# Earlier accumulating transfers, a seven-product group in the first block, and a twelfth group with sums made ahead, in a one-core decoder layer

## The chip, the core and the metric

The kernel runs on one core of one Trainium2 chip. A core has a matrix engine (TensorE, PE in the profile), a vector engine (VectorE, DVE), a scalar engine (ScalarE, ACT), a general engine (GpSimd, POOL), a sequencer that here issues nearly all loads (SyncE, SP), and sixteen engines for transfers (DMA) which all queues share. Each engine works through its own list of instructions in the order in which the program was written down, and waits on semaphores for the others. The metric is device microseconds of one execution, lower is better.

## The reference

One decoder layer over 256 tokens of width 2048, all in float32: a half feed-forward with a residual and a norm, two token mixers side by side (retention in chunks, and attention over a window with sinks), their gated mix, a second half feed-forward, and a gated embedding. Cut to what matters here:

```python
D_MODEL, SEQ, D_FF = 2048, 256, 5632

def swiglu(x, w_gu, w_down):
    g, u = jnp.split(x @ w_gu, 2, axis=-1)
    return (jax.nn.silu(g) * u) @ w_down

def reference(x, p, positions, ...):
    h = x
    h = layer_norm(alpha * h + 0.5 * swiglu(h, w_ffn1_gu, w_ffn1_down), ...)
    rq, rk, rv, rg, aq, ak, av, gate_r, gate_a = jnp.split(h @ w_in, SPLIT_POINTS, axis=-1)
    ro = head_group_norm(retention_chunkwise(rotary(rq), rotary(rk) * DK ** -0.5, rv), ret_gn_g)
    ret_branch = (jax.nn.silu(rg) * ro) @ w_ret_out
    att_branch = sliding_window_attention_sinks(rotary(aq), rotary(ak), av, att_sinks) @ w_att_out
    mixed = (jax.nn.sigmoid(gate_r) * ret_branch + jax.nn.sigmoid(gate_a) * att_branch) @ w_mix_out
    h = layer_norm(alpha * h + mixed, ...)
    h = layer_norm(alpha * h + 0.5 * swiglu(h, w_ffn2_gu, w_ffn2_down), ...)
    ple = jax.nn.sigmoid(h @ w_ple_gate) * (p @ w_ple_proj)
    return layer_norm(alpha * h + ple, ...)
```

`w_gu` is 2048 by 11264 and `w_down` 5632 by 2048, once for each feed-forward. Every weight is read once, so the work is a stream of weights past 256 tokens.

## The kernel before

**Three matmuls for one product.** Float32 numbers are split in two parts, hi and lo, of a shorter type (`F32R`). One product of two tiles is then three matmuls: lo of the activations with hi of the weights (L431), hi with hi (L432), hi of the activations with lo of the weights (L433). A matmul has 128 rows of tokens on one side and 512 columns of weights on the other.

**Weights.** A weight chunk is 128 by 1024 numbers, 512 KB (tile `r...`, loaded by SP at L119). The split is a copy on ACT to `h...` (L105) and a subtraction on DVE to `l...` (L106). In the tile names `lf1_gu_2_1_6`, the letter is lo, `f1_gu` is the gate and up projection of feed-forward 1, block 2, half 1 (0 is gate, 1 is up), pair 6 of features.

**Blocks and units.** The gate and up projections are made in 11 blocks (0 to 10) of 512 gate and 512 up columns. A block is a sum over eight units, one for each pair of feature tiles. A unit has one of four kinds:

- P: two chunks, each split as above. 8 products, 24 matmuls.
- F: like P, but the second chunk is *folded*: its lo is not subtracted on DVE. ACT writes minus the raw chunk into it (L169, one multiplication), POOL issues a transfer that adds the raw chunk to it (L170, `lf_gu<-rf_gu`, 512 KB), and ACT copies hi (L171). The accumulating transfer takes the place of the rounding subtraction that DVE would have made.
- S: the *seven*: seven products in place of eight, in the manner of Strassen, 21 matmuls. DVE makes four sums of weight halves (L226 to L229, tiles `u` and `v`), and three splits follow on ACT and DVE (`h`, `b`, `hu`, `hv` and the same with `l`). A block with sevens needs four further banks of PSUM (`f1..s0` to `s3`) and, at its end, the *fold*: a copy on ACT (`eve`, L549) and four operations on DVE (`evw`, `eve`, L550 to L553), then the four sums that add in the block's own banks (L1056), the activation (L1057) and the product. A block without sevens ends with activation (L1062) and product (L1064) alone. The activations for sevens are sums too (`sums`, L504 to L507, split into `f1fh` and `f1fl`), made once.
- D: a seven whose sums of weights were made in an earlier stage, stored in DRAM (`sums_ahead`) and loaded again.

Feed-forward 1 is PPPPPPPP in block 0 and FFSSFSSP in the other ten. The units' pairs are fixed, sevens are pairs 0 to 3, and folded chunks are pairs 4, 5 and 6. Feed-forward 2 has five sevens in each of its blocks 1 to 7, one or two of them of kind D, and four sevens in blocks 8 to 10. The down projections are made in two parts with lists of their own, `FIRST_DOWN` and `SECOND_DOWN`, one letter for each of 22 units.

**What sets the order.** Units stand in one list, `plan`. `fill()` runs whenever a unit has been multiplied: it loads the next units and makes them (the split) as long as slots are free (`room["slots"]`, of a pool of 46) and the units waiting amount to less than 45 (made) or 90 (loaded) units of matmul time, 12 for a chunk and 21 for a seven. So the lists of SP, ACT, DVE and POOL follow the order of `plan`, some units ahead of the matmuls, and a folded chunk's multiplication, its accumulating transfer and its hi copy are written at one place (`Folded.make`), in turn with the units around it. In block 0 of feed-forward 1 the four chunks of `x` are loaded between the weights (`first_chunk`), and the number of slots is raised to 24 before its seventh unit. Work for other stages (`sums_ahead`) is put in small steps between the units (`lazy`).

Of the kernel before, what the change touches and what calls it, by code (L numbers as in the profile page):

```python
# [38 lines left out]
SLOTS = 46  # L39


SEVEN = (0, 1, 2, 3)

AHEAD = {1: (4, 5), 2: (4,), 3: (4, 5), 4: (4,), 5: (4, 5), 6: (4,), 7: (4, 5)}
AHEAD_SLOTS = 36

DELAY = 1

SEVEN_DOWN = (6, 7, 8, 9)

FIRST_DOWN = "PPPPPPFFSFSPSFSPSFSSPS"
SECOND_DOWN = "PPPSPSPSFSPSFSSPSPPPPP"
LEAD = 4

# [8 lines left out]
def layer(ctx: ExitStack, tc: tile.TileContext, io):  # L63
# [87 lines left out]
        def make(self):  # L151
            self.chunk.make()

    class Folded:

        loads, makes, keeps, time = 1, 2, 2, 12

        def __init__(self, key):  # L160
            self.key = key

        def load(self, **how):
            self.chunk = Chunk(self.key, **how)

        def make(self):
            c = self.chunk
            c.make_hi()
            act.mul(c.lo, c.raw, -1.0)  # L169
            pool.dma_start(c.lo, c.raw, accum_op=ALU.add)  # L170
            act.copy(c.hi, c.raw)  # L171

    class Turn:

# [141 lines left out]
    def fill(must=False):  # L316

        while True:
            queued = sum(u.time for u in ready)
            left = room["slots"] - room["used"]  # L320
            wanted = must and not ready or not room["quiet"] and queued < room["ahead"]
            if loaded and wanted and loaded[0].makes <= left:
                u = loaded.pop(0)
                u.make()
                room["used"] += u.keeps - u.loads
                ready.append(u)
                continue
            first = loaded[0] if loaded else plan[0] if plan else None
            queued += sum(u.time for u in loaded)
            if plan and queued < room["far"] and plan[0].loads + first.makes <= left:  # L330
                u = plan.pop(0)
                u.load()
                room["used"] += u.loads
                loaded.append(u)
                continue
            return

    def make_next():
# [4 lines left out]
        ready.append(u)  # L343

    def take(key):
        if not ready:
            fill(True)
        u = ready.pop(0)
        assert u.key == key, (u.key, key)
        return u  # L350
# [102 lines left out]
    def block_units(units, keys):  # L453

        for kind, p in units:
            if kind == "P":
                plan.extend(Single(keys(n, p)) for n in range(2))
            elif kind == "F":
                plan.extend(of(keys(n, p)) for n, of in enumerate((Single, Folded)))
            else:  # L460
                plan.append((Seven if kind == "S" else Prepared)(keys(0, p), keys(1, p)))

# [511 lines left out]
    def ffn(name, i, ht, norm, keep, residual, keepers, away):  # L974
# [33 lines left out]
        for j in range(KF // 4):  # L1008
# [22 lines left out]
            def before(u, j=j, offset=KD // 2 - len(units)):  # L1031
                u += offset
                if j == 0 and norm is None and u % 2 == 0:
                    first_chunk(u // 2)
                    if u == 6:
                        slots_for_weights(24)
                    if u == 2:
                        load_constants()
                if j == 0 and u == 7:
                    for g in sorted({p // 2 for p in SEVEN}):  # L1040
                        hi, lo = (slot([P, 8, P], F32R, f"{name}f{w}{g}") for w in "hl")
                        made[g] = seven_forms(keep[g], hi, lo)
                    if name == "f2":
                        g = AHEAD[1][0] // 2
# [169 lines left out]
    def mixers(ht, norm, residual, keepers, away):  # L1214
# [295 lines left out]

        made = {}
        forms = lambda p: made[p // 2](p % 2)
        lazy.append(sums_ahead(ahead[6:9], 2, 2))
        slots_for_weights(18)
        sig = []
        for j in range(4):
# [76 lines left out]

        lhs = lambda k: of_pairs(mix_t, k)
        slots_for_weights(16)
        lazy.append(sums_ahead(ahead[9:], 3, 2))

        def residual_added(blk, ps):
            for t in range(2):
# [344 lines left out]
```

## Time and profile before

| | |
|---|---|
| median of 3 runs | 2230.45 us (2227.97 to 2230.84) |
| profiled execution | 2230.62 us, of which the profile's span is 2228.6 us |
| PE, share of the span busy | 100% (2218.5 us) |
| DVE | 90% (2004.0 us) |
| ACT | 65% (1439.0 us) |
| POOL | 2% (50.9 us) |
| mean traffic to and from the memory | 233 GB/s |
| granted clock of the matrix engine | 0.999 |

A page of the profile gives busy times, the chain of work that ended last, and groups of instructions. The list of waits names, for each engine, what a waiting instruction was released by. A timeline row has the start, the duration, the engine, the line, the operation, its output and inputs, and in square brackets how long the engine sat idle before it and what ended that. A matmul row says 0.39 us, but matmuls overlap: what counts is the distance between the starts of two of them. Of the queues, q1 carries the loads that SP issues, and q0 the accumulating transfers that POOL issues.

### The profile page before, as it was taken

How to read it: one execution, taken by the hardware profiler on the slowest of the kernel's cores; microseconds unless marked ns; L12 is line 12 of the kernel's file. 1: busy time of each engine (PE TensorE's matmuls, PEld its weight loads, DVE VectorE, ACT ScalarE, POOL GpSimd, SP SyncE). 2: the span in 40 equal slices, each digit the busy share in tenths (PEclk: the TensorE clock that was granted, in tenths of full speed). 3: DMA queues.
4: the chain of work that ended last, by engine and by line, in shares of the span. 5: the costliest groups of instructions: out<-in, count | busy, mean ns of one | idle time of the engine just before them, and what ended most of it. 6: DMA issues, size and time to landing. Idle time of an engine off the chain costs nothing.

```text
span 2228.6 us, 29103 instructions
## 1 busy us (share of the span) xinstructions
PE 2218.5 (100%) x10140; PEld 1838.9 (83%) x10140; DVE 2004.0 (90%) x2624; ACT 1439.0 (65%) x1677; POOL 50.9 (2%) x65
## 2 busy tenths in 40 slices
PE   9999999999999999999999999999999999999998
PEld 8888888888888888888788888888888888888887
DVE  6999999989998789789999888779999999999977
ACT  6777777777565545557865567466766677765653
POOL 0000000000000000000000000000000000000000
PEclk9999999999999999999999999999999999999999
DMA  9988998976686889757976568888999999666871
GB/s 321 250 264 252 249 263 241 269 227 217 228 305 234 298 283 338 203 179 232 291 233 226 184 203 321 316 302 266 301 301 295 300 248 276 209 233 221 309 283 68
DMA packets 302075, 570.51 MB, mean 256 GB/s; under 512 B 98652, under 2 KB 103388, under 8 KB 301928
## 3 DMA queue, kind: packets, MB, share of 16 engines
q1 hardware_dynamic: 291880, 536.71, 72.3%
q0 software_dynamic: 8064, 29.36, 7.0%
q10 hardware_dynamic: 1984, 2.58, 0.4%
q8 instruction: 79, 1.29, 0.2%
q14 instruction: 68, 0.56, 0.1%
HBM read 487.32 MB, written 31.46 MB: 233 GB/s over the span
## 4 chain that ended last, share of the span: by engine, by line
PE 93%; DMA 3%; DVE 2%; issue 1%; ACT 0%; SPq 0%; ACTq 0%; POOL 0%; DVEq 0%; POOLq 0%
PE rqk L382 3%; PE f2g L431 3%; PE f2g L433 3%; PE f2g L432 3%; PE f1g L431 2%; PE f1g L433 2%; PE f1g L432 2%; PE f2u L431 2%; PE f2u L433 2%; PE f2u L432 2%; PE f1u L433 2%; PE f1u L431 2%; PE f1u L432 2%; PE aqk L382 2%; PE f2e L431 1%; PE f1e L431 1%
## 5 line engine op out<-in xcount | busy, mean ns | idle before, releaser
L106 DVE TENSOR_TENSOR lf_gu<-rf_gu,hf_gu 128x1024 fp32r<-128x1024 f32 (+1 forms) x225 | 267.7, 1210 | 22.1 <-ACT hf_gu L105 21.1
L105 ACT CAST hf_gu<-rf_gu 128x1024 fp32r<-128x1024 f32 (+1 forms) x225 | 228.7, 1039 | 22.1 <-DMA rf_gu<-in_f_gu 21.5
L106 DVE TENSOR_TENSOR lw_in_f<-rw_in_f,hw_in_f 128x1024 fp32r<-128x1024 f32 x140 | 167.8, 1219 | 15.0 <-ACT hw_in_f L105 15.0
L106 DVE TENSOR_TENSOR lf_down<-rf_down,hf_down 128x1024 fp32r<-128x1024 f32 x130 | 155.7, 1220 | 12.9 <-ACT hf_down L105 11.1
L105 ACT CAST huf_gu<-uf_gu 128x1024 fp32r<-128x1024 f32 x76 | 80.1, 1053 | 125.4 <-DVE uf_gu L227 109.4
L105 ACT CAST hf_down<-rf_down 128x1024 fp32r<-128x1024 f32 x130 | 132.7, 1049 | 30.5 <-DMA rf_down<-in_f_down 21.3
L105 ACT CAST hw_in_f<-rw_in_f 128x1024 fp32r<-128x1024 f32 x140 | 140.4, 1049 | 2.3 <-PE gt L433 1.6
L105 ACT CAST hvf_gu<-vf_gu 128x1024 fp32r<-128x1024 f32 x76 | 80.1, 1054 | 32.4 <-DVE vf_gu L229 30.5
L106 DVE TENSOR_TENSOR luf_gu<-uf_gu,huf_gu 128x1024 fp32r<-128x1024 f32 x76 | 92.6, 1218 | 0.0
L106 DVE TENSOR_TENSOR lvf_gu<-vf_gu,hvf_gu 128x1024 fp32r<-128x1024 f32 x76 | 92.6, 1218 | 0.0
L431 PE MATMUL f1g<-hf_gu,xt 128*128 128x512 f32 x232 | 90.8, 391 | 0.0
L433 PE MATMUL f1g<-lf_gu,xt 128*128 128x512 f32 x232 | 90.5, 390 | 0.0
L432 PE MATMUL f1g<-hf_gu,xt 128*128 128x512 f32 x232 | 90.5, 390 | 0.0
L431 PE MATMUL f2g<-hf_gu,ht 128*128 128x512 f32 x211 | 82.2, 390 | 0.0
L433 PE MATMUL f2g<-lf_gu,ht 128*128 128x512 f32 x211 | 82.1, 389 | 0.0
L432 PE MATMUL f2g<-hf_gu,ht 128*128 128x512 f32 x211 | 82.1, 389 | 0.0
L433 PE MATMUL f1u<-lf_gu,xt 128*128 128x512 f32 x192 | 75.0, 391 | 1.2 <-DMA lf_gu<-rf_gu 1.2
L431 PE MATMUL f1u<-hf_gu,xt 128*128 128x512 f32 x192 | 74.7, 389 | 0.0
L432 PE MATMUL f1u<-hf_gu,xt 128*128 128x512 f32 x192 | 74.7, 389 | 0.0
L170 POOL DMA_DIRECT2D lf_gu<-rf_gu x42 | 36.4, 867 | 1641.2 <-DMA rf_gu<-in_f_gu 1017.6
L105 ACT CAST huf_down<-uf_down 128x1024 fp32r<-128x1024 f32 x32 | 33.7, 1054 | 60.7 <-DVE uf_down L227 58.7
L1057 ACT ACTIVATE eve<-eve 128x1024 f32<-128x1024 f32 x20 | 21.2, 1061 | 67.3 <-DVE eve L1056 67.3
(1512 smaller groups left out, 6978.3 us busy)
## 6 DMA issues: line engine op xcount, KB each, us to landing
rf_gu<-in_f_gu SPq DMA_DIRECT2D x361, 512.0 KB
rf_down<-in_f_down SPq DMA_DIRECT2D x176, 512.0 KB
rw_in_f<-in_w_in_f SPq DMA_DIRECT2D x148, 512.0 KB
lf_gu<-rf_gu POOLq DMA_DIRECT2D x42, 512.0 KB, 8.2
rw_rv<-in_w_rv SPq DMA_DIRECT2D x32, 512.0 KB
rw_ret<-in_w_ret SPq DMA_DIRECT2D x32, 512.0 KB
rw_mix<-in_w_mix SPq DMA_DIRECT2D x32, 512.0 KB
rw_pg<-in_w_pg SPq DMA_DIRECT2D x32, 512.0 KB
```

The costliest lines, as they stand in the source:

```text
L105: act.copy(dst_hi, src)
L106: (lo_engine or dve).tensor_tensor(dst_lo, src, dst_hi, ALU.subtract)
L170: pool.dma_start(c.lo, c.raw, accum_op=ALU.add)
L382: pe.matmul(ps[f], hi[:, kk, f * P : (f + 1) * P], rhs(k), start=k == 0, stop=k == n_k - 1,)
L431: pe.matmul(o, al, bh, start=first, stop=False)
L432: pe.matmul(o, ah, bh, start=False, stop=False)
L433: pe.matmul(o, ah, bl, start=False, stop=self.left == 0)
L1057: act.activation(g, g, AF.Silu)
```

## The change

It has five parts.

1. *Folded chunks in two steps.* `Folding` loads the chunk, multiplies and issues the accumulating transfer; it counts no matmul time and is put into `plan` at least 12 units of time ahead of the place where the chunk is used, and further back to ahead of a seven if one stands within the twelve entries ahead of that place. `Folded` at the old place only copies hi. This is done for every folded chunk, of the down projections too.
2. *Block 0 of feed-forward 1* takes its pairs in the order 0, 1, 4, 5, 6, 7, 2, 3, and the last of them, pair 3, is a seven. The chunks of `x` are loaded in the order 0, 2, 3, 1, the sums of activations for pairs 2 and 3 (`f1f..1`) are made ahead of unit 6 and those for pairs 0 and 1 (`f1f..0`) ahead of unit 7, and the slots are raised in two steps.
3. *Block 1 of feed-forward 1* is FFSSFSSF in place of FFSSFSSP: one folded chunk more.
4. *`FIRST_DOWN`*, used in both feed-forwards, has eight sevens as before in other places, six folded chunks in place of five, and eight units P in place of nine.
5. *Block 8 of feed-forward 2* is PFSSDSSP in place of PFSSFSSP, with the pair 4 as the seven whose sums are made ahead. In retention's stage `sums_ahead` makes four groups in its second run in place of three; the other runs make as many as before.

```diff
+FOLD_AHEAD = 12, 12
+FORMS_AT = {"f1": {6: (1,), 7: (0,)}, "f2": {7: (0, 1, 2)}}
+FIRST_SLOTS = {4: 16, 6: 28}
+X_ORDER = (0, 2, 3, 1)
-AHEAD = {1: (4, 5), 2: (4,), 3: (4, 5), 4: (4,), 5: (4, 5), 6: (4,), 7: (4, 5)}
+AHEAD = {1: (4, 5), 2: (4,), 3: (4, 5), 4: (4,), 5: (4, 5), 6: (4,), 7: (4, 5), 8: (4,)}
+FIRST_UNITS = {
+    "f1": [('P', 0), ('P', 1), ('P', 4), ('P', 5), ('P', 6), ('P', 7), ('P', 2), ('S', 3)],
...
-FIRST_DOWN = "PPPPPPFFSFSPSFSPSFSSPS"
+FIRST_DOWN = "PPPPPFFSFSFSPSFSPSFSPS"
...
-    class Folded:
-        loads, makes, keeps, time = 1, 2, 2, 12
+    class Folding:
+        loads, makes, keeps, time = 1, 1, 2, 0
...
+        def load(self):
+            self.chunk = Chunk(self.key)
         def make(self):
             c = self.chunk
-            c.make_hi()
+            c.lo = slot(list(c.raw.shape), F32R, "l" + c.name)
             act.mul(c.lo, c.raw, -1.0)
             pool.dma_start(c.lo, c.raw, accum_op=ALU.add)
+    class Folded:
+        loads, makes, keeps, time = 0, 1, 2, 12
...
+        def make(self):
+            c = self.chunk = self.begun.chunk
+            c.hi = slot(list(c.raw.shape), F32R, "h" + c.name)
             act.copy(c.hi, c.raw)
+            room["used"] -= self.begun.keeps
+    def fold_at(ahead, key):
+        begun = Folding(key)
+        at, time = len(plan), 0
+        while at > 0 and time < ahead:
+            at -= 1
+            time += plan[at].time
+        if ahead and any(isinstance(u, Seven) for u in plan[at - 12 : at + 1]):
+            while not isinstance(plan[at], Seven):
+                at -= 1
+        plan.insert(at, begun)
+        plan.append(Folded(begun))
...
     def gu_units(name, j):
         if j == 0:
-            return [("P", p) for p in range(KD // 2)]
+            return FIRST_UNITS[name]
...
+        if name == "f1" and j == 1:
+            return units_of("FFSSFSSF", SEVEN)
...
-                    if u == 6:
-                        slots_for_weights(24)
+                    if u in FIRST_SLOTS:
+                        slots_for_weights(FIRST_SLOTS[u])
...
-        lazy.append(sums_ahead(ahead[3:6], 2, 2))
+        lazy.append(sums_ahead(ahead[3:7], 2, 2))
...
-            load_x_chunk(c + 1)
+            load_x_chunk(X_ORDER[c + 1])
```

The lines of the kernel move down by 13 (L106 becomes L119) to 41 (L1056 becomes L1097); L550 becomes L590.

How the lists of instructions move is shown at three places. The first is ACT at the end of block 0 of feed-forward 1. Before, these rows are the splits of the activations' sums (`f1fh`), the first two units of block 1 (`..1_0_5`, `..1_1_5`), the activation of block 0 (`f1v0`) and the first seven of block 1 (`..1_0_0`):

```order
L105 CAST f1fh0_438<-sums_440 128x1024
L105 CAST f1fh1_447<-sums_449 128x1024
L105 CAST hf1_gu_1_0_5_468<-rf1_gu_1_0_5_413 128x1024
L169 ACTIVATE lf1_gu_1_1_5_489<-rf1_gu_1_1_5_415 128x1024
L171 CAST hf1_gu_1_1_5_488<-rf1_gu_1_1_5_415 128x1024
L1062 ACTIVATE f1v0_493<-f1g00_117 128x512
L1062 ACTIVATE f1v0_493<-f1g01_118 128x512
L105 CAST hf1_gu_1_0_0_524<-rf1_gu_1_0_0_417 128x1024
```

The same place of the change; `eve_509<-f10s0` is the copy that begins the fold of block 0:

```order
L118 CAST hf1_gu_1_0_4_443<-rf1_gu_1_0_4_353 128x1024
L198 CAST hf1_gu_1_1_4_465<-rf1_gu_1_1_4_345 128x1024
L118 CAST f1fh0_467<-sums_469 128x1024
L118 CAST hf1_gu_1_0_5_497<-rf1_gu_1_0_5_447 128x1024
L198 CAST hf1_gu_1_1_5_501<-rf1_gu_1_1_5_347 128x1024
L589 COPY eve_509<-f10s0_121 128x512
L1098 ACTIVATE eve_509<-eve_509 128x1024
L118 CAST hf1_gu_1_0_0_548<-rf1_gu_1_0_0_449 128x1024
```

The multiplications for the two folded chunks are gone from here (they stand further ahead now), one of the two splits of sums too, and the copy out of the bank `f10s0` is new.

The second is DVE at the same place. Before, block 0 ends with two products, and the sums of block 1's first seven follow:

```order
L106 TENSOR_TENSOR f1fl1_448<-sums_449,f1fh1_447 128x1024
L106 TENSOR_TENSOR lf1_gu_1_0_5_469<-rf1_gu_1_0_5_413,hf1_gu_1_0_5_468 128x1024
L1064 TENSOR_TENSOR f1v0_493<-f1v0_493,f1u00_119 128x512
L1064 TENSOR_TENSOR f1v0_493<-f1v0_493,f1u01_120 128x512
L226 TENSOR_TENSOR uf1_gu_1_0_0_518<-rf1_gu_1_0_0_417,rf1_gu_1_1_0_419 128x512
```

In the change nine operations stand between the same two neighbours:

```order
L119 TENSOR_TENSOR f1fl0_468<-sums_469,f1fh0_467 128x1024
L119 TENSOR_TENSOR lf1_gu_1_0_5_498<-rf1_gu_1_0_5_447,hf1_gu_1_0_5_497 128x1024
L590 TENSOR_TENSOR evw_510<-eve_509,f10s1_122 128x512
L591 TENSOR_TENSOR eve_509<-evw_510,f10s2_123 128x512
L592 TENSOR_TENSOR evw_510<-f10s3_124,evw_510 128x512
L593 TENSOR_TENSOR evw_510<-f10s3_124,eve_509 128x512
L1097 TENSOR_TENSOR eve_509<-eve_509,f1g00_117 128x512
L1097 TENSOR_TENSOR eve_509<-eve_509,f1g01_118 128x512
L1097 TENSOR_TENSOR evw_510<-evw_510,f1u00_119 128x512
L1097 TENSOR_TENSOR evw_510<-evw_510,f1u01_120 128x512
L1099 TENSOR_TENSOR evw_510<-eve_509,evw_510 128x1024
L267 TENSOR_TENSOR uf1_gu_1_0_0_542<-rf1_gu_1_0_0_449,rf1_gu_1_1_0_451 128x512
```

The fold and the five operations behind it took the place of two products.

The third is ACT in block 1, from the third folded chunk (`..1_1_6`) to the block's last seven (`..1_0_3`). Before:

```order
L169 ACTIVATE lf1_gu_1_1_6_639<-rf1_gu_1_1_6_553 128x1024
L171 CAST hf1_gu_1_1_6_638<-rf1_gu_1_1_6_553 128x1024
L105 CAST hf1_gu_1_0_2_672<-rf1_gu_1_0_2_591 128x1024
L105 CAST bf1_gu_1_0_2_676<-rf1_gu_1_1_2_593 128x512
L105 CAST huf1_gu_1_0_2_679<-uf1_gu_1_0_2_666 128x1024
L105 CAST hvf1_gu_1_0_2_683<-vf1_gu_1_0_2_667 128x1024
L105 CAST hf1_gu_1_0_3_707<-rf1_gu_1_0_3_611 128x1024
```

And in the change:

```order
L198 CAST hf1_gu_1_1_6_669<-rf1_gu_1_1_6_503 128x1024
L118 CAST hf1_gu_1_0_2_700<-rf1_gu_1_0_2_616 128x1024
L118 CAST bf1_gu_1_0_2_704<-rf1_gu_1_1_2_618 128x512
L118 CAST huf1_gu_1_0_2_707<-uf1_gu_1_0_2_694 128x1024
L118 CAST hvf1_gu_1_0_2_711<-vf1_gu_1_0_2_695 128x1024
L181 ACTIVATE lf1_gu_1_1_7_727<-rf1_gu_1_1_7_636 128x1024
L181 ACTIVATE lf1_gu_2_1_4_730<-rf1_gu_2_1_4_638 128x1024
L181 ACTIVATE lf1_gu_2_1_5_733<-rf1_gu_2_1_5_640 128x1024
L118 CAST hf1_gu_1_0_3_742<-rf1_gu_1_0_3_642 128x1024
```

The multiplication for `..1_1_6` has moved up (to ahead of the casts of the seven `..1_0_1`), and the three multiplications for block 1's last unit and block 2's first two now stand ahead of the last seven's casts. The transfers on POOL's list follow the same order.

More of the change, by code (lines that the diff above doesn't have):

```diff
@@ L322, in fill @@
             if loaded and wanted and loaded[0].makes <= left:
[L323 to L326, printed above, removed]
+                make_next()
                 continue
@@ L342, in make_next @@
         room["used"] += u.keeps - u.loads
-        ready.append(u)
+        if u.time:
+            ready.append(u)
     def take(key):
-        if not ready:
+        while not ready:
             fill(True)
@@ L458, in block_units @@
             elif kind == "F":
-                plan.extend(of(keys(n, p)) for n, of in enumerate((Single, Folded)))
+                plan.append(Single(keys(0, p)))
+                fold_at(FOLD_AHEAD[keys(1, p)[0][-3:] == "_gu"], keys(1, p))
             else:
@@ L1512, in mixers @@
         forms = lambda p: made[p // 2](p % 2)
-        lazy.append(sums_ahead(ahead[6:9], 2, 2))
+        lazy.append(sums_ahead(ahead[7:10], 2, 2))
         slots_for_weights(18)
@@ L1595, in mixers @@
         slots_for_weights(16)
-        lazy.append(sums_ahead(ahead[9:], 3, 2))
+        lazy.append(sums_ahead(ahead[10:], 3, 2))
         def residual_added(blk, ps):
```

15 lines of the change are left out of this document (9 added, 6 removed).

## The prediction

> **What bounds the kernel now.** I read the page first, then the list of waits, then windows, and the timeline where a wait stands.
>
> ```profile
> span 2228.6 us, 29103 instructions
> ...
> PE 2218.5 (100%) x10140; PEld 1838.9 (83%) x10140; DVE 2004.0 (90%) x2624; ACT 1439.0 (65%) x1677; POOL 50.9 (2%) x65
> ...
> PE 93%; DMA 3%; DVE 2%; issue 1%; ACT 0%; SPq 0%; ACTq 0%; POOL 0%; DVEq 0%; POOLq 0%
> ```
>
> PE is busy all the time and carries 93% of the chain that ended last. So there are two ways to gain: fewer matmuls, or fewer of the waits that still interrupt them. The list of waits says how much there is:
>
> ```profile
> PE f1u L433 <- DMA lf_gu<-rf_gu: 1.2, 2, 0.9
> PE f1e L431 <- DVE evw L550: 0.6, 1, 0.6
> PE mr1a L433 <- DVE lw_ret L106: 0.5, 1, 0.5
> PE f2e L431 <- DVE evw L550: 0.5, 1, 0.5
> ```
>
> The change touches three of these four rows: two waits for an accumulating transfer, and one in each down projection for the fold. None is longer than 1 us. The windows give the price of a matmul, and how full DVE is:
>
> ```profile
> 0.00:56.00 56.00, 54.63 (x238) 45.23 (x239) 38.90 (x48) 36.75 (x42) 2.58 (x8) 1.00 0.97 321
> 336.00:392.00 56.00, 56.00 (x249) 46.37 (x248) 53.21 (x66) 41.70 (x46) 2.59 (x3) 1.00 0.87 248
> 830.00:877.00 47.00, 47.00 (x211) 39.03 (x211) 45.94 (x69) 24.95 (x30) 0.00 (x0) 1.00 0.96 346
> 877.00:910.00 33.00, 33.00 (x157) 27.73 (x157) 27.80 (x56) 16.98 (x20) 0.00 (x0) 1.00 0.85 258
> ```
>
> The columns are the window, PE, its weight loads, DVE, ACT, POOL, the clock, the share of DMA and GB/s. In the steady blocks of feed-forward 1 (second row) 249 matmuls take 56.00 us, or 0.2267 us each between two starts with rounding of the count, and DVE is busy for 53.21 of 56. DVE is nearly as full as PE, so what is put on DVE in front of a seven can become a wait of PE. At the start (first row) DMA is 97% busy.
>
> **Fewer matmuls.** Two pairs become sevens, in block 0 of feed-forward 1 and in block 8 of feed-forward 2: 2 x (24 - 21) = 6 matmuls, 6 x 0.2267 = 1.36 us less. This term is certain unless a wait takes it.
>
> **The accumulating transfers (part 1).** The two waits in the timeline of PE:
>
> ```profile
> 73.43 0.39 PE L432 MATMUL f1u<-hf_gu,xt 128*128 128x512 f32 x1
> 74.70 0.50 PE L433 MATMUL f1u<-lf_gu,xt 128*128 128x512 f32 x1 [0.88 <-DMA lf_gu<-rf_gu]
> ...
> 237.81 0.39 PE L432 MATMUL f1u<-hf_gu,xt 128*128 128x512 f32 x1
> 238.54 0.50 PE L433 MATMUL f1u<-lf_gu,xt 128*128 128x512 f32 x1 [0.34 <-DMA lf_gu<-rf_gu]
> ...
> 574.81 0.39 PE L433 MATMUL f1e<-lf_down,f1ah 128*128 128x512 f32 x1
> 575.79 0.50 PE L431 MATMUL f1e<-hf_down,f1al 128*128 128x512 f32 x1 [0.59 <-DVE evw L550]
> ```
>
> From start to start it takes 1.27 and 0.73 us in place of 0.23, so they cost 1.04 + 0.50 = 1.5 us. The chain shows why:
>
> ```profile
> 63.73 10.93 DMA lf_gu<-rf_gu
> ```
>
> The transfer is issued at 63.73 and lands 10.93 us later. In the change it stands ahead of the casts of the seven two units earlier, with the seven (21 matmuls) and more between: at least 21 x 0.2267 = 4.8 us sooner, and the wait was 1 us. I take all of the 1.5 us (bounds 0.5, if the load of the raw chunk or the queue of ACT eats a part, and 1.5). Nothing is late next there: the lo of the next seven on DVE had been ready for some us.
>
> Where the transfers are begun sooner they meet other loads. What the queues do after the first one is issued, in the timeline of POOL and in two stretches of the view of transfers:
>
> ```profile
> 39.39 1.01 POOL L170 DMA_DIRECT2D lf_gu<-rf_gu  x1 [38.08 <-ACT lf_gu L169]
> ```
>
> ```profile
> q1 hardware_dynamic: 902, 1.75, 104.6%
> ```
>
> ```profile
> q0 software_dynamic: 133, 0.52, 74.3%
> q1 hardware_dynamic: 206, 0.39, 32.2%
> ```
>
> The first stretch is 39.0 to 43.5 us: the loads (q1) have all engines and q0 has no row. The second is 43.5 to 47.0 us: now the accumulating transfer takes 74% and the loads fall to 32%. So it was served behind the loads already queued. In the change the two first transfers are issued some 4 us sooner or more, in the stretch where block 0 waits for loads, and by this row they still come behind the loads queued before, those of the new seven among them. Cost 0, with an upper bound in the rivals. The Trainium skill ("DMA: Bandwidth & Descriptors", Queues, rings and completion order) says otherwise: each engine takes turns between the rows of queues that have work, packet by packet. By that rule the sum would be the rival's 2234.7 us; this row of the trace doesn't bear it out.
>
> **The end of block 0 (part 2).** This is the largest new cost. What DVE, PE and ACT do there before:
>
> ```profile
> 43.88 0.43 DVE L507 TENSOR_TENSOR sums<-xraw,sums 128x256 f32<-128x256 f32 x1
> 45.47 1.23 DVE L106 TENSOR_TENSOR f1fl<-sums,f1fh 128x1024 fp32r<-128x1024 f32 x1 [1.17 <-ACT f1fh L105]
> 46.62 1.22 DVE L106 TENSOR_TENSOR lf_gu<-rf_gu,hf_gu 128x1024 fp32r<-128x1024 f32 x1
> 49.68 1.37 DVE L1064 TENSOR_TENSOR f1v<-f1v,f1u 128x512 f32<-128x512 f32 x2 [1.84 <-PE f1u L433]
> 50.96 0.68 DVE L226 TENSOR_TENSOR uf_gu<-rf_gu,rf_gu 128x512 f32<-128x512 f32 x1
> ...
> 56.49 1.22 DVE L106 TENSOR_TENSOR lvf_gu<-vf_gu,hvf_gu 128x1024 fp32r<-128x1024 f32 x1
> 57.63 0.68 DVE L226 TENSOR_TENSOR uf_gu<-rf_gu,rf_gu 128x512 f32<-128x512 f32 x1
> ```
>
> ```profile
> 50.09 0.39 PE L431 MATMUL f1g<-hf_gu,xt 128*128 128x512 f32 x1
> ```
>
> ```profile
> 38.01 1.06 ACT L169 ACTIVATE lf_gu<-rf_gu 128x1024 fp32r<-128x1024 f32 x1 [0.28 <-DMA rf_gu<-in_f_gu]
> ```
>
> A seven takes DVE from 50.96 to 57.63, 6.67 us. Its second chunk is the 22nd row of loads on SP in the change; before, the 22nd is the one that landed when ACT began at 38.01. So DVE starts the new seven at about 38.6 and ends at 45.3. PE came to block 1 at 50.09; with 3 matmuls fewer it is 49.41. PE thus begins the new seven 21 matmuls earlier, at 44.65, and uses its parts one after the other: no wait, or under 1 us.
>
> Behind the seven DVE has one subtraction (1.14, the distance of 45.47 and 46.62), the four sums of activations (0.43 each by the row, 1.6 with their overlap), a round trip to ACT (1.17) and two subtractions (2.3): to 51.5. ACT, whose rows are in the part on the change, makes the split of these sums (from 48.1, a cast is 1.05), two more casts, and then the copy that frees bank `f10s0`: end at about 51.6. The first matmul of block 1 writes into that bank. It would start at 49.41 and starts at 51.6: **2.2 us lost**. Before, block 1's banks were free. The lower bound is 0.6 us, the wait that the fold causes in the down projection (row of 575.79, the same pattern of a block that ends in a seven); the upper is 3.6 us, if the seven's second chunk lands one load (1.35 us) later. I take 2.2, by the rows of the same place.
>
> Then the fold (4 x 0.65; the row of 50.96 has 0.68, a little less from start to start) and five operations (4 x 0.65 and 1.14) stand ahead of block 1's first seven: DVE begins it at 51.6 + 2.6 + 2.6 + 1.1 = 57.9, and the second at 64.6. Its first lo is ready after four sums and a subtraction, 2.65 + 1.14, at 68.4. PE begins block 1 at 51.6, has 48 + 21 matmuls (15.6 us) ahead of the second seven, and wants its lo as the third matmul: 67.7. That is **0.6 us lost** (bounds 0 and 1.5; before, these were ready some 5 us early). The sevens behind a folded unit gain 24 matmuls of PE time against 1.1 us of DVE, and I see no wait there; block 1's one subtraction fewer (part 3) helps what follows.
>
> **FIRST_DOWN (part 4).** The wait at 574.81 costs 0.98 - 0.23 = 0.75 us, its twin in feed-forward 2 by the list of waits (0.5 against 0.6) about 0.65. What delayed the fold is a row of DVE:
>
> ```profile
> 563.84 0.69 DVE L226 TENSOR_TENSOR uf_down<-rf_down,rf_down 128x512 f32<-128x512 f32 x1 [3.29 <-DMA rf_down<-in_f_down]
> ```
>
> DVE waited 3.29 us for the load of a seven. In the lists of instructions this load's slot is let go 58 matmuls ahead of its use before, and 76 in the change: 18 x 0.2267 = 4.1 us sooner. DVE also has one subtraction fewer (1.14). Both are more than the 0.75 us needed. I take the whole 1.4 us (bounds 0 and 1.4).
>
> **Retention and block 8 (part 5).** Four sums and two subtractions, 4 x 0.65 + 2 x 1.14 = 4.9 us on DVE, two casts on ACT, 1 MB of loads and 2 MB of stores. Placed in 830 to 877 they would collide (DVE 45.94 of 47, DMA 0.96), but they fall in 877 to 910, where DVE has 5.2 us idle and DMA is at 0.85. Cost 0, bounds 0 and 1. Block 8 then looks like blocks 2, 4 and 6 of the same stage, which have no row in the list of waits: 0, bounds 0 and 1.
>
> **Sum.** -1.36 - 1.5 - 1.4 + 2.2 + 0.6 = -1.5 us. Against the profiled execution's 2230.62 us that is **2229.1 us**; the median of the runs, 2230.45, is 0.2 lower and within their spread of 2.9 us.
>
> **Rivals.**
>
> *The end of block 0 is covered.* If loads land earlier and ACT comes to the copy sooner, the cost is 0.6 in place of 2.8: 2227.0 us. For it: DVE had 1.84 us idle ahead of 49.68. Against: the new work there is longer than that.
>
> *The transfers push in front of the loads (slower).* If the two first transfers get the engines at once, each holds back the loads of 3.5 us by two thirds, 4.8 us in all, as in the stretch from 43.5. The seven's chunk lands near 42.8, its sums cost PE about 1.3 us, and the copy ends near 57 against 51.6: 5.5 us more than forecast, 2234.7. It is slower than before as soon as the chunk lands over 1.5 us late. Against: the row of 39.0 to 43.5. The page of the Trainium skill named above would have it so.
>
> *Multiplications bunch on ACT (slower).* In blocks 1 to 9 two or three of them stand ahead of the last seven's casts. What room there is:
>
> ```profile
> 120.92 1.22 DVE L106 TENSOR_TENSOR lvf_gu<-vf_gu,hvf_gu 128x1024 fp32r<-128x1024 f32 x1
> ```
>
> ```profile
> 124.48 0.39 PE L433 MATMUL f12s<-lvf_gu,f1fh 128*128 128x512 f32 x1
> ```
>
> The last part is ready at 122.14 and used at 124.48: 2.3 us. Two multiplications (1.06 each by the row of 38.01, 1.9 with their overlap) fit by 0.4 even if ACT has no idle time. From there on each 0.5 us more, as by a raw chunk that lands late and holds up ACT, costs 9 x 0.5 = 4.5 us: 2233.6. Against: ACT is idle for 14 of 56 us in the steady window.
>
> *The waits only move.* Parts 1 and 4 gain nothing since the next thing is late: 2230.62 - 1.36 + 2.8 = 2232.1.
>
> **Chances.** The forecast 0.55 (its own range 2227.5 to 2231), block 0 covered 0.17, transfers in front 0.08, ACT bunching 0.08, waits only move 0.12. A measurement can tell 0.2%, 4.5 us, from no change: below 2226.0 or above 2234.9. Only the outer halves of the first rival (with 0.3 to 1 us of small gains that I don't see) and of the two slower ones lie there: faster 0.10, same 0.83, slower 0.07. Range 2225.6 to 2234.0.
>
> **What would show it.** Right: no wait of PE for `lf_gu<-rf_gu`, none for `evw` in the down projections, a wait of about 2 us of the first matmul of block 1 for ACT's `eve`, and a small one for a lo of its second seven. Wrong: a wait of PE inside the new seven (the loads are late), many small waits in the last sevens of blocks 1 to 9 (ACT), or waits of PE at 880 to 950 (retention's sums).

## The result, and the profile after

The change made the kernel slower: 2233.91 us median (2231.0 to 2244.95), against 2228.32 us (2226.1 to 2233.15) for the kernel before, twelve runs of each. The ratio, taken over all runs and not from the medians, is 1.0031, with a 95% interval of 1.0023 to 1.0040. The profiled execution took 2232.59 us, its span is 2230.8 us. Two things about these numbers matter below. The profile of before, on which the prediction's sum rested, was one of its longer executions (2230.62 us against a median of 2228.32). And the runs of the change lie over 14 us, those of before over 7.

The page of the change (values of the same rows as before):

```profile
span 2230.8 us, 29165 instructions
...
PE 2217.3 (99%) x10134; PEld 1837.4 (82%) x10134; DVE 2013.6 (90%) x2641; ACT 1443.7 (65%) x1683; POOL 52.6 (2%) x67
...
PE 87%; DVE 6%; DMA 4%; issue 2%; ACT 1%; SPq 0%; ACTq 0%; DVEq 0%; POOLq 0%
```

PE has 6 matmuls fewer and is busy 1.2 us less, but the span is 2.2 us longer, and DVE and DMA carry 10% of the chain in place of 5%. The list of waits of PE:

```profile
PE f1u L472 <- DMA lf_gu<-rf_gu: 2.5, 1, 2.5
PE f1g L470 <- ACT eve L589: 1.8, 1, 1.8
...
PE f11s L472 <- DVE lf_gu L119: 0.6, 1, 0.6
PE f26s L472 <- DVE luf_gu L119: 0.4, 1, 0.4
PE f11s L472 <- DVE luf_gu L119: 0.3, 1, 0.3
```

The two waits for the fold in the down projections are gone. The wait for an accumulating transfer is not gone: there is one of 2.5 us where there were two of together 1.2. New are the wait for `eve` at the end of block 0 and small ones in sevens.

By stage, from the first matmul into a bank in both traces: at block 2's first seven the change is 1.84 us behind (104.79 against 102.95), at block 6's 3.99, at the second half of the first down projection 3.29 (so 0.9 was won in the first half), and at the mix 2.18, 1.1 less, because a wait for `lw_ret` that no part touches happened not to occur. It is 3.30 behind at block 7 of feed-forward 2 and 2.62 at block 9, after the three matmuls fewer. The two places that cost most, in the timeline of PE:

```profile
48.82 0.39 PE L472 MATMUL f1g<-lvf_gu,xt 128*128 128x512 f32 x1
50.96 0.50 PE L470 MATMUL f1g<-hf_gu,xt 128*128 128x512 f32 x1 [1.75 <-ACT eve L589]
...
239.65 0.39 PE L471 MATMUL f1u<-hf_gu,xt 128*128 128x512 f32 x1
242.52 0.50 PE L472 MATMUL f1u<-lf_gu,xt 128*128 128x512 f32 x1 [2.48 <-DMA lf_gu<-rf_gu]
```

Start to start these are 2.14 and 2.87 us in place of 0.23. The second is the odd one: this transfer was begun 4 us sooner than its counterpart before, and yet it is later. The chain gives its length, first in the kernel before and then in the change:

```profile
229.58 8.92 DMA lf_gu<-rf_gu
```

```profile
225.54 16.93 DMA lf_gu<-rf_gu
```

Before it was issued at 229.58 and had landed by 238.50; now it is issued at 225.54 and lands at 242.47. ACT shows what stands around the issue. Before, and then in the change:

```profile
220.39 1.99 ACT L185 COPY wf<-evw 128x1024 uint16<-128x1024 uint16 x2
...
228.02 1.06 ACT L169 ACTIVATE lf_gu<-rf_gu 128x1024 fp32r<-128x1024 f32 x1
```

```profile
222.23 1.99 ACT L226 COPY wf<-evw 128x1024 uint16<-128x1024 uint16 x2
224.12 1.06 ACT L181 ACTIVATE lf_gu<-rf_gu 128x1024 fp32r<-128x1024 f32 x1
```

`wf` is the block's result, cut in 16-bit words, which SP then moves with a transposing transfer (`mf<-wf`). Before, five casts, of the next seven and its neighbour, stood between `wf` and the multiplication. Now the two follow each other, so the transposing transfer and the accumulating one are issued within a microsecond (224.90 and 225.54). What the queues did then (packets, MB, share of the 16 engines), 228 to 240 us of the change:

```profile
q1 hardware_dynamic: 2235, 0.85, 90.6%
q0 software_dynamic: 95, 0.35, 37.5%
```

And the same transposing transfer before, 224 to 229 us:

```profile
q1 hardware_dynamic: 2312, 0.96, 115.0%
```

The 2048 packets of 256 bytes of a transposing transfer took 2.6 to 4.7 us in each of the ten blocks before, with at most 15 packets of q0 among them. In the change they took 9.7, 8.4 and 13.1 us in blocks 3, 4 and 5, with 88 to 128 packets of q0 among them. Meeting alone does not make them slow, though: in block 9 there were 118 such packets, and the transposing transfer took 6.3 us. In the 12 us of block 5 shown above both queues together moved 1.2 MB, 100 GB/s, while the engines were counted busy all the time.

### The profile page after: what moved, and what is told of

It is laid out like the page before. It is cut to its first block, busy times and chain, and to the rows that moved or that the text cites. A ratio compares the mean times of both kernels' runs of the same rounds, so it can differ in the third digit from the quotient of the medians.

```text
span 2230.8 us, 29165 instructions
## 1 busy us (share of the span) xinstructions
PE 2217.3 (99%) x10134; PEld 1837.4 (82%) x10134; DVE 2013.6 (90%) x2641; ACT 1443.7 (65%) x1683; POOL 52.6 (2%) x67
## 4 chain that ended last, share of the span: by engine, by line
PE 87%; DVE 6%; DMA 4%; issue 2%; ACT 1%; SPq 0%; ACTq 0%; DVEq 0%; POOLq 0%
PE rqk L421 3%; PE f2g L470 2%; PE f2g L472 2%; PE f2g L471 2%; PE f2u L470 2%; PE f2u L472 2%; PE f2u L471 2%; PE f1g L470 2%; PE f1g L471 2%; PE f1g L472 2%; PE aqk L421 2%; DMA rf_gu<-in_f_gu 2%; PE f1u L472 1%; PE f1u L470 1%; PE f1u L471 1%
## 5 line engine op out<-in xcount | busy, mean ns | idle before, releaser
L119 DVE TENSOR_TENSOR lf_gu<-rf_gu,hf_gu 128x1024 fp32r<-128x1024 f32 (+1 forms) x223 | 266.2, 1210 | 31.3 <-ACT hf_gu L118 30.3
L119 DVE TENSOR_TENSOR lw_in_f<-rw_in_f,hw_in_f 128x1024 fp32r<-128x1024 f32 x140 | 167.9, 1220 | 14.2 <-ACT hw_in_f L118 13.8
L119 DVE TENSOR_TENSOR lf_down<-rf_down,hf_down 128x1024 fp32r<-128x1024 f32 x128 | 153.9, 1220 | 15.6 <-ACT hf_down L118 13.7
L119 DVE TENSOR_TENSOR luf_gu<-uf_gu,huf_gu 128x1024 fp32r<-128x1024 f32 x77 | 93.9, 1219 | 0.0
L119 DVE TENSOR_TENSOR lvf_gu<-vf_gu,hvf_gu 128x1024 fp32r<-128x1024 f32 x77 | 93.8, 1218 | 0.0
```

What stands on the lines that cost most here:

```text
L119: (lo_engine or dve).tensor_tensor(dst_lo, src, dst_hi, ALU.subtract)
```

## The experiments

Theory A: an accumulating and a transposing transfer that run at one time make each other slow, and how badly differs from run to run. Theory B: the seven in block 0 is the loss. Theory C: a lower clock that has nothing to do with the parts. All times are medians. The kernel before was run beside them: 2227.09 us for the first four experiments, 2228.35 for the next four and 2228.64 for the last four.

**Part 1 undone.**

```diff
-FOLD_AHEAD = 12, 12
+FOLD_AHEAD = 0, 0
```

> The change with its first part undone: each accumulating transfer is issued where it was before (FOLD_AHEAD 0, 0); the other four parts stay. Theory A, the transfers begun sooner meet the transposing transfers of the block before and both become slow, by an amount that differs from run to run: the wait of 2.5 us for lf_gu<-rf_gu in block 5 goes, the waits of 1.0 and 0.5 us of before come back, the waits at the end of block 0 and in block 1 (1.9, 1.0 and 1.0 us) stay; median about 2229 to 2231 us, and the spread of the runs shrinks from 14 us to some 5. Theory B, the loss is that of the new seven in block 0 (3.8 us in all): the time stays near 2233 us. Theory C, a lower granted clock in a part of the runs that has nothing to do with the parts: the same spread as the change, 2231 to 2245.

Measured: 2246.09 us (2241.98 to 2251.16), ratio 1.0085 (1.0073 to 1.0097). All theories missed: it is 12 us slower than the change, not faster. Its waits:

```profile
PE f1d L472 <- DMA lf_down<-rf_down: 4.3, 2, 3.8
PE f1u L472 <- DMA lf_gu<-rf_gu: 3.1, 4, 1.1
PE f1g L470 <- ACT eve L589: 2.7, 1, 2.7
PE f10s L470 <- DVE f1fl L119: 1.5, 1, 1.5
```

The other parts lean on the first: with the new lists the folded chunks come too late without an earlier start, in the down projection above all, and in block 0 the split of the activations' sums then comes too late for the seven itself.

**Parts 2 and 3 undone.**

```diff
-    "f1": [('P', 0), ('P', 1), ('P', 4), ('P', 5), ('P', 6), ('P', 7), ('P', 2), ('S', 3)],
+    "f1": [('P', 0), ('P', 1), ('P', 2), ('P', 3), ('P', 4), ('P', 5), ('P', 6), ('P', 7)],
-FORMS_AT = {"f1": {6: (1,), 7: (0,)}, ...
+FORMS_AT = {"f1": {7: (0, 1)}, ...
-FIRST_SLOTS = {4: 16, 6: 28}
+FIRST_SLOTS = {6: 24}
-X_ORDER = (0, 2, 3, 1)
+X_ORDER = (0, 1, 2, 3)
-            return units_of("FFSSFSSF", SEVEN)
+            return units_of("FFSSFSSP", SEVEN)
```

> The change with its second and third part undone (block 0 of feed-forward 1 without a seven, the chunks of x and the slots as before, block 1 with its last unit plain); the transfers begun sooner, the new list of the down projection and the twelfth group of sums stay. Theory A: the waits of block 0 and block 1 are gone, the waits for lf_gu<-rf_gu stay and differ from run to run; median 2229 to 2232, with a spread of some 10 us. Theory B: 3 matmuls fewer (0.7), two waits for transfers (1.5) and two for the fold (1.4) gone: about 2225 against a before of 2228.3, with a spread of some 5 us. Theory C: the spread of the change.

Measured: 2244.25 us (2237.52 to 2266.81), ratio 1.0087 (1.0052 to 1.0121). Theory B falls in its plain form: the seven is gone and the kernel is slower. Theory A has the sign and the spread, but is too low by 12 us. The profiled run (2256.95 us) has waits for `lf_gu<-rf_gu` of together 8.8 us in three places, and behind them the splits of sevens on DVE are late too:

```profile
PE f1u L472 <- DMA lf_gu<-rf_gu: 8.8, 3, 4.7
PE f11s L472 <- DVE lf_gu L119: 5.0, 1, 5.0
```

**Part 1 alone**, on the kernel before: as in the last one, and with `FIRST_DOWN`, `AHEAD` and the slices of `sums_ahead` as before.

> The kernel before with the first part alone: accumulating transfers begun sooner, all else as before. Theory A: slower than before by 2 to 4 us, 2230 to 2232, with runs up to 2240. Theory B: faster by the two waits, 1.5 us: 2226.8. Theory C: as before in its fast runs, with some runs 5 to 10 us longer at a clock of 0.997.

Measured: 2244.66 us (2237.01 to 2269.74), ratio 1.0095 (1.0059 to 1.0131). So the part that was to remove two waits costs 17.6 us by itself. The profiled run has one wait for `lf_gu<-rf_gu`, from 318 us on in block 7, and the seven behind it is late by another 2.5:

```profile
PE f1u L472 <- DMA lf_gu<-rf_gu: 8.7, 1, 8.7
```

It also shows something that is in no theory. Windows of that run (columns as above, the granted clock is the third from the right):

```profile
327.00:332.00 5.00, 5.00 (x12) 3.94 (x13) 0.00 (x0) 0.00 (x0) 0.00 (x0) 0.50 1.07 264
332.00:336.00 4.00, 4.00 (x19) 3.24 (x18) 1.28 (x2) 1.67 (x2) 0.00 (x0) 0.97 1.03 368
```

After the wait PE ran at half clock for 5 us: 11 matmuls 0.43 us apart in place of 0.23, another 2.2 us. That is what lowers the mean clock of the long runs (0.993 to 0.998 here, 0.999 before). Theory C has cause and effect the wrong way round: the waits lower the clock. Here the record of the clock falls to half at 322.0 us, 3.7 us after the wait began.

**Parts 4 and 5 alone**, on the kernel before.

> The kernel before with the fourth and fifth part alone (the new list of the down projection, and the twelfth group of sums in retention with five sevens in block 8). Theories A and B agree: 3 matmuls fewer (0.7) and the two waits for the fold (0.75 and 0.68) gone, so 2.1 us faster than before, 2226.2; the added work in retention costs nothing. If that work costs something, waits of PE at 700 to 950 us.

Measured: 2234.6 us (2230.92 to 2239.59), ratio 1.0034 (1.0022 to 1.0046); 2 us faster was expected. Its longest waits:

```profile
PE f1d L472 <- DMA lf_down<-rf_down: 3.0, 1, 3.0
PE f2d L472 <- DMA lf_down<-rf_down: 1.5, 1, 1.5
```

The waits for the fold are gone, as expected, but in each down projection one for a folded chunk took their place. The new list needs part 1 in the down projections. PE has no wait at 700 to 950 us: the twelfth group of sums costs nothing that this profile shows.

**The collision, made in the kernel before.** The turning of a block's result (the copies `wf` and the transposing transfer behind them) comes two units later, next to the multiplication; no accumulating transfer changes its place among the units:

```diff
-            later(1, lambda j=j, v=v: turned(j, v))
+            later(3, lambda j=j, v=v: turned(j, v))
```

> The kernel before, with one number changed: the turning of a block's result (two copies to wf on ACT and the transposing transfer behind them) comes two units later, so that it stands right ahead of the multiplication of the third folded chunk, as it does in the change; no accumulating transfer is moved. Theory A, accumulating and transposing transfers that run at one time make each other slow: waits of PE for lf_gu<-rf_gu of 2 to 9 us in some blocks, stretches of some 10 us in which both queues are busy at under 60 GB/s, median 2235 to 2245 against 2227. Theory B2, the earlier issue as such does the harm (the loads behind it are held back): as before, 2227, no long wait.

Measured: 2249.53 us (2241.11 to 2255.07), ratio 1.0091 (1.0074 to 1.0107). 21 us are lost without a transfer begun sooner, but not all by the collision.

```profile
PE f1u L433 <- DMA lf_gu<-rf_gu: 15.7, 9, 9.6
PE f2u L433 <- DMA lf_gu<-rf_gu: 2.4, 3, 1.4
```

Nine of the ten blocks with folded chunks wait. The worst waits 9.6 us; there the transposing transfer took 14 us, the accumulating one landed 16.5 us after its issue, and in the stretch from 401 to 412 us both queues together moved 109 GB/s:

```profile
q1 hardware_dynamic: 2194, 0.86, 101.7%
q0 software_dynamic: 89, 0.33, 33.0%
```

That block is theory A's. In the other eight, with together 6.1 us of waits, the transposing transfer took its ordinary 2.6 to 4.6 us and the accumulating one landed in 7.2 to 8.4 us, as before (5.1 to 10.9). It was late there because the edit also brought its issue closer to its use, 6.9 us ahead in place of 8.6.

**The change, with the turning two units later** (the same edit, in both feed-forwards).

> The change, with the turning of a block's result two units later, behind the first seven after the early multiplication, so that the accumulating transfer has gone when the transposing one comes. Theory A: the wait of 2.5 us in block 5 goes in all runs, the runs lie together within some 4 us, and what stays is block 0 (3.8 us) less the gains: about 2229 us. Theory B2: as the change, 2234 with runs to 2245.

Measured: 2250.72 us (2243.79 to 2261.84), ratio 1.0105 (1.0081 to 1.0129). Missed, and yet it speaks for A: in feed-forward 1 no wait for `lf_gu<-rf_gu` is left. The collision has moved to feed-forward 2, whose order differs. In its worst place SP issued the transposing transfer at 1765.48 and POOL an accumulating one at 1766.58. ACT, whose next casts need loads that queue behind them, sat idle for 15.74 us, and with it the copy that frees a bank:

```profile
PE f2g L470 <- ACT eve L589: 10.1, 2, 9.5
```

**The change, without the move to ahead of a seven.** The third multiplication then stands behind the casts of the first seven again, as before:

```diff
-        if ahead and any(isinstance(u, Seven) for u in plan[at - 12 : at + 1]):
+        if False and any(isinstance(u, Seven) for u in plan[at - 12 : at + 1]):
```

> The change, but an accumulating transfer is begun 12 units of time ahead and is not moved further back to ahead of a seven; on ACT the third multiplication then stands five casts behind wf, one cast sooner than before. Theory A: no long wait for lf_gu<-rf_gu, the runs lie together, about 2229 us (block 0 costs 3.8, the gains are 1.4 of matmuls, 1.5 and 1.4 of waits, against 2227). Theory B2: between before and the change, 2231.

Measured: 2243.84 us (2241.82 to 2247.39), ratio 1.0068 (1.0056 to 1.008). The spread shrank from 14 to 6 us, as A has it, and no wait for `lf_gu<-rf_gu` is over 1.3 us; but the median is 15 us too high. In its profile PE waits 3.4 us for `eve`, and in the down projections 3.2 and 1.4 us for folded chunks: these needed the move.

**The same, with blocks 0 and 1 as before.**

> The same, with blocks 0 and 1 of feed-forward 1 as before: transfers begun 12 units of time ahead, the new list of the down projection, and the twelfth group of sums. Theory A: all gains and no loss: 0.7 of matmuls, up to 1.5 and 1.4 of waits: 2223.5 to 2225, faster than both kernels. Theory B2: 2229.

Measured: 2231.73 us (2229.98 to 2237.42), ratio 1.0018 (1.0009 to 1.0026); 7 us more than expected. No wait for `lf_gu<-rf_gu` is left, which is what A said; those in the down projections remain, and half clock behind the first:

```profile
PE f1d L472 <- DMA lf_down<-rf_down: 1.8, 1, 1.8
PE f2d L472 <- DMA lf_down<-rf_down: 1.6, 1, 1.6
```

**The move only in the down projections**, where no result is turned, and blocks 0 and 1 as before:

```diff
-        if ahead and any(isinstance(u, Seven) for u in plan[at - 12 : at + 1]):
+        if ahead and not key[0].endswith("_gu") and any(isinstance(u, Seven) for u in plan[at - 12 : at + 1]):
```

> Blocks 0 and 1 of feed-forward 1 as before, the new list of the down projection, the twelfth group of sums, and transfers begun 12 units of time ahead; moved back to ahead of a seven only in the down projections, where no result is turned, and not in the gate and up projections. Theory A: the waits for lf_down<-rf_down of the same kernel without that move (1.8 and 1.6 us, with the slow clock behind them 2.0 and 1.8) go, no wait for lf_gu<-rf_gu comes back: 2231.7 - 4 = about 2227.5, at or just below the kernel before. If the median stays above 2230, something is missing in theory A.

Measured: 2226.1 us (2224.98 to 2228.9) against 2228.64, ratio 0.999 (0.9981 to 0.9998). It is faster than both kernels, by 2.5 us than the one before and by 6.2 than the change (run again beside it, the last experiment), and its runs lie within 4 us. All that is left in the list of waits:

```profile
PE warm L1863 <- POOL ident masks.py:199: 1.4, 1, 1.4
PE pln L1749 <- DVE plnst L1747: 0.2, 1, 0.2
PE mr1s L472 <- DVE lvw_ret L119: 0.2, 1, 0.2
```

**The change, with the turning two units later in feed-forward 1 alone.**

```diff
-            later(1, lambda j=j, v=v: turned(j, v))
+            later(3 if name == "f1" else 1, lambda j=j, v=v: turned(j, v))
```

> The change, with the turning of a block's result two units later in feed-forward 1 alone, where its transposing transfer then comes some 9 us behind the early accumulating one. Theory A: no long wait for lf_gu<-rf_gu in feed-forward 1; in feed-forward 2 as the change; block 0 and 1 keep their 3.8 us: about 2230 to 2231, the runs within 5 us. Against A: runs spread to 2245 as in the change.

Measured: 2230.9 us (2229.53 to 2232.67), ratio 1.0011 (1.0002 to 1.002). As theory A had it: no wait for `lf_gu<-rf_gu` in either feed-forward, the spread falls from 14 to 3 us, and its transposing transfers take 2.4 to 4.1 us again. What stays is block 0, the start and block 1:

```profile
PE f1g L470 <- ACT eve L589: 1.4, 1, 1.4
PE warm L1863 <- POOL ident masks.py:199: 1.4, 1, 1.4
PE f1g L470 <- ACT hf_gu L118: 0.8, 1, 0.8
PE f11s L472 <- DVE lf_gu L119: 0.6, 1, 0.6
PE f11s L472 <- DVE luf_gu L119: 0.4, 1, 0.4
```

**The move only in the down projections, with blocks 0 and 1 as in the change.**

> The change, with accumulating transfers moved back to ahead of a seven only in the down projections; blocks 0 and 1 of feed-forward 1 as in the change. Its difference to the same kernel with those blocks as before is what parts 2 and 3 cost. Theory A with the waits at the end of block 0 and in block 1 (1.9 to 3.4, and 1 us): 2 to 4 us slower than that one, less 0.7 for three matmuls. Theory B, in a form that is left: the seven in block 0 is the larger part of the loss of the change, over 5 us.

Measured: 2235.21 us (2233.44 to 2237.06), ratio 1.0028 (1.0017 to 1.004). It is 9.1 us slower than the same kernel with plain blocks, so theory A's 2 to 4 us are missed, and theory B in the form that was left (over 5 us) is met in this kernel. The wait for `eve` is 3.4 us, PE then runs at a clock of 0.58 for 4 us (7 matmuls 0.43 us apart), and the third folded chunk of block 1 comes 2.0 us late:

```profile
PE f1g L470 <- ACT eve L589: 3.4, 1, 3.4
PE f1u L472 <- DMA lf_gu<-rf_gu: 2.2, 2, 2.0
```

**The change again.**

> The change once more, beside the kernel before on the same chip as the other experiments. Theory A: the same waits at the end of block 0 and in block 1, and waits for lf_gu<-rf_gu in other blocks and of other lengths than in the first profile, since two queues meet by chance; median 2232 to 2240. A theory by which the waits are set by the order alone: the wait of 2.5 us in block 5 again and nowhere else.

Measured: 2232.25 us (2229.84 to 2242.87), ratio 1.0023 (1.0012 to 1.0034). The profiled run (2242.73 us) waits at other places than the first: none in block 5, but 3.7 us in block 3 (issued at 145.50, landing 18.16 us later) and 2.2 us in block 4, each followed by half clock:

```profile
PE f1u L472 <- DMA lf_gu<-rf_gu: 5.9, 2, 3.7
```

The order alone doesn't set these waits. The wait for `eve` is 2.9 us this time, and here too the clock falls:

```profile
52.50:56.50 4.00, 3.95 (x10) 3.19 (x11) 3.85 (x8) 0.00 (x0) 0.00 (x0) 0.57 1.04 322
```

## Why the prediction was wrong

The forecast was 2229.1 us, 1.5 us less than the profiled execution; it became 5.6 us more by the medians. The 2233.91 us lie just inside the forecast's range, but the change went the other way. By stage, the forecast's terms against what the first profile shows (us, start to start):

| stage | forecast | profile |
|---|---|---|
| feed-forward 1, blocks 0 and 1 | +1.08 | +1.84 |
| block 5 (the accumulating transfer) | -0.50 | +2.15 |
| its other blocks | 0 | +0.19 |
| first down projection | -0.75 | -0.89 |
| the mix (no part touches it) | 0 | -1.11 |
| feed-forward 2, block 6 | 0 | +1.12 |
| block 8 | -0.68 | -0.68 |
| second down projection | -0.65 | -0.80 |
| together | -1.5 | +1.8 |

So in this profile block 5 is 2.65 of the 3.3 us that were missed. Point by point:

- **Fewer matmuls**, -1.36 us: right. They are gone, and the three of block 8 are worth the 0.68 us that they were priced at.
- **The accumulating transfers**, -1.5 us: this step failed, and in the first profile it is the main one. It said that the transfer stands ahead of a seven's casts now, that nothing is late next, and that it comes behind the loads already queued, at cost 0. I counted the loads it was moved past and not the transposing transfer on SP's queue, whose copies (`wf`) stand right ahead of the new place. The runs show this in both directions: bringing the two together in the kernel before costs up to 21 us (9.6 us of wait in the one block that collided in its profile), and taking them apart in the change wins 1.4 us in the median (2230.9 against 2232.25), 3.5 in the mean, and up to 12 in single runs. In the rival "the transfers push in front of the loads" the mechanism was near, with the wrong partner, the wrong place and a chance of 0.08; that its 2234.7 us lie close to the measured time is chance.
- **What the row of 39.0 to 43.5 us says.** I read it as order between queues: loads first. It only shows that q0 had not started yet: its first packet came at 43.74 us, 4.35 us after the issue, and whether loads or something else held it the row does not say. From then on, where q0 had 74% and q1 32%, both ran at once. The rule of the Trainium skill ("DMA: Bandwidth & Descriptors", Queues, rings and completion order), turns between rows of queues packet by packet, agrees with the stretch of 228 to 240 us, where both queues had work and both moved. The rule doesn't say that the sum of both would fall to 100 GB/s.
- **The end of block 0**, +2.2 us: the mechanism and the size were right for the first profile (2.14 - 0.23 = 1.9): ACT waits 3.6 us for the sums, makes three casts, and then `eve` frees the bank. In other runs the wait for `eve` was 1.4 to 3.4 us. The second step that failed is that I took the wait as the whole price: where it was 2.4 us or longer, PE then ran at half clock for 6 to 13 matmuls, 1.2 to 2.6 us more.
- **Block 1**, +0.6 us in the second seven: 0.75 measured. That the later sevens would not wait was wrong: the last one waited 1.0 us (0.73 and 0.57 in place of 0.23 each, and the slower matmuls behind them). An `hf_gu` at the very start was late too in some runs (0.8). Parts 2 and 3 together, forecast at 2.8 - 0.7 = 2.1 us, cost 9.1 and 12.1 us in the two pairs of experiments that differ in them alone and move nothing ahead of a seven in the gate and up projections (2235.21 against 2226.1, 2243.84 against 2231.73); there `eve` came 3.4 us late with half clock behind it. With that move, as in the change, the same two parts are a gain: the change is 5.6 us above the kernel before, and without them 17.2.
- **FIRST_DOWN**, -1.4 us: right, both waits for the fold are gone; but only together with part 1 in the down projections. Without it the new list, with part 5, is 7.5 us slower than before.
- **Retention and block 8**, 0: right in retention. In block 6 of feed-forward 2, PE waited for `luf_gu` and `lvf_gu`, 1.1 us from start to start, which the variants without the move to ahead of a seven don't show: the rival of multiplications that bunch on ACT may be there, in one block and at a quarter of its price.
- **The base.** The sum was made against an execution 2 us above the median. The kernel's own small waits differ from run to run, and one profile shows one draw of them. The best variant is 4.3 us shorter than before by the profiles' spans, but 2.5 us by the medians.

By the medians of the last four experiments the weights are others. The gains without the collision and without parts 2 and 3 are 2.5 us (the move only in the down projections, against the kernel before). From there to the change with its turning later it is 4.8 us more, and from there to the change 1.4. The 4.8 are not parts 2 and 3 alone, since the two kernels also differ in where the gate and up transfers begin and in the turning; but the profile of the change with its turning later has hardly another wait than those of blocks 0 and 1 and of the start. So these are the larger loss in the median, and the collision is what makes single runs up to 10 us longer than the rest.

What stays open: why the collision is harder without the seven in block 0 (17.6 us in the kernel with part 1 alone, 1 to 3 in the change), though the order on ACT is the same there. The traces show where to look, as the last section says: it depends on which of the two transfers is issued first, and on how much of the transposing one is still to go. No run holds this still.

## What to carry to other kernels

When a transfer is moved sooner, look at what else it will now run beside, on all queues and with its kind: count the transposing transfers too, not only the loads. A wait of a few microseconds on the matrix engine has a second bill, the clock behind it. And parts of a change can hold each other up: the new list of the down projection was a loss without the earlier start and a gain with it, so a single part's worth is not its worth in the whole.

## What the runs showed of the hardware

A transposing transfer here is 2048 packets of 256 bytes. Of the 308 that turn the feed-forwards' results in the 14 traces, 226 had no packet of an accumulating transfer among theirs, and took 2.2 to 5.9 us. Fourteen took over 7 us, up to 18.1. Each of these had 88 to 148 of the accumulating transfer's packets of 4096 bytes among its own, and the accumulating transfer then took 10.3 to 23.1 us from issue to landing, in place of 5.1 to 10.9 before. Meanwhile all queues together moved 75 to 151 GB/s, though the engines were counted busy. Fourteen others had 41 to 118 such packets among them and took only 4.0 to 6.4 us. What divides the two kinds in these traces: in all the slow ones the accumulating transfer was issued behind the transposing one, and its first packet came with 432 or more of the 2048 still to go; in the others it was issued first, or came with 199 or fewer to go. No run tests this order by itself.

After each of the 14 waits of PE of 2.6 us and more in these traces the granted clock was 0.5 for some matmuls, most often 7 (5 to 13, but 3 in one case), 0.427 us apart in place of 0.227; so it was after 4 of the 7 waits between 1.8 and 2.5 us, and after none of the shorter ones. Except at the very end of the program, the records of the clock hold 0.5 for 3.41, 6.83 or 10.24 us at a time. The Trainium skill ("TensorE: Matmul & The Clock Gate", Part 1: The HAM clock gate) has it that the clock halves after an idle window of about 3.4 us, and that the windows run free of the program. The length of the records agrees. So does the chance in it, that the clock fell after a wait of 1.8 us and not after one of 2.5. The waits that were enough were shorter here than a window, down to 1.8 us.
